# The gate weights of an mLSTM: high and low parts in one tile instead of two

## The chip, the cores and the metric

The kernel runs on one core of one Trainium2 chip. The core has five engines with instruction streams of their own: TensorE (matmuls; its weight loads are shown apart), VectorE, ScalarE, GpSimd and SyncE. They share an on-chip memory, and TensorE writes to accumulator banks. Transfers are issued from the queues of SyncE, ScalarE and GpSimd and are moved by 16 DMA engines. The metric is the time of one execution on the device in microseconds (us), as the median of several.

## The reference

The reference is an encoder trunk of two layers over 256 tokens of width 1024. Each layer is a SwiGLU block, a mixer and another SwiGLU block, each added to its input and normalised. The mixer of the first layer is a bidirectional mLSTM, that of the second a windowed attention. What the change touches is in the mLSTM:

```python
def mlstm_mixer(x, w_in, gate_b, norm_g, w_out):
    p = x @ w_in
    q, k, v, o = ...                     # columns 0 to 3071 of p
    gates = (p[..., 3072:] + gate_b)     # 16 columns: (i, f) x two directions x 4 heads
    h_f = mlstm_chunkwise(q, k, v, gates[0], gates[1])
    h_b = flip(mlstm_chunkwise(flip(q), flip(k), flip(v), flip(gates[2]), flip(gates[3])))
    ...
# in mlstm_chunkwise
    logf = log_sigmoid(f_pre)            # the forget gate, summed along the tokens
    g = cumsum(logf)
    # the input gate i_pre - g and its running maximum weight the scores q k
```

So 16 of the projection's columns are gates; from them come, token after token, the weights of the scores and a stabiliser.

## The kernel before, in words

All matrix products are in float32 precision out of three products in a faster format: each operand is split into a high part (a rounded copy, written by ScalarE) and a low part (the rest, written by VectorE), and `mm3` (lines 619 to 622) adds high by high, high by low and low by high in one bank. The weights come from memory in pieces of 128 x 1024 numbers, over four buffers; for each piece ScalarE writes `w_hi` and VectorE `w_lo`. The profile shows these operations under line 182, the line of the helper through which TensorE, VectorE and ScalarE are called, so one tells them apart by tiles.

The order of the instructions on each engine is written out by the program. In the SwiGLU blocks `Weights.fill` (line 378) decides by modelled times (class `Paced`) when the next piece is split; in the mLSTM the places are fixed by calls of `W.done`. SyncE loads the next piece as soon as a `w_lo` has freed a buffer.

The mLSTM (line 1056) holds the input turned round in `xT` (1024 numbers in 8 strips of 128, by 256 tokens, high and low). Its order is:

- GpSimd clears two weight tiles for the gates, `gw_hi` and `gw_lo` (128 x 8 x 128 each, lines 1065 to 1067). The 16 gate columns of `gw` are split into them (line 1070): the four heads of each gate stand at columns 0, 32, 64 and 96, the rest is zero. So one matmul with these weights lays each gate on partitions of its own.
- v of the first 128 tokens (lines 1090 to 1097), with the turning of the second 128 tokens of the block before put between (`pending`).
- The gates (lines 1099 to 1101): `mm3` for 8 strips, 24 matmuls, into one bank `pg` of 128 x 256.
- The gate chain on VectorE (lines 1102 to 1130): three steps read the bank and add the bias, then come the log-sigmoid (with Exp and Ln on ScalarE), two running sums, `u`, two running maxima, and `ex`. Two small transfers on GpSimd's queue put the maxima into `most` (line 1128).
- Meanwhile TensorE computes v of the second 128 tokens (lines 1132 to 1136); with each half go a split of v and the splits of two more weight pieces.
- Four transposes of `u` and `ex` on TensorE (lines 1138 to 1141), then q and k (lines 1171 to 1185), where GpSimd spreads `most` over the partitions, and after that scores, mixing and the output projection.

`v_lo`, `q_lo` and `w_lo` are low parts written by VectorE; `scan` holds the tiles `fa`, `fe`, `fl` and `fm` of the gate chain, `ig` its input gate. In the rows of the profile both the gate bank and other banks of that pool are called `pw`, those of a second pool `py`.

Of the kernel before, what the change touches and what calls it, by code (L numbers as in the profile page):

```python
# [9 lines left out]
F32 = mybir.dt.float32  # L10
FR = mybir.dt.float32r
AF = mybir.ActivationFunctionType
OP = mybir.AluOpType
# [177 lines left out]
class Weights:  # L191
# [134 lines left out]
    def low(self):  # L326

        nc = self.nc
        i, hi = self.half.pop(0)
        p = self.plan[i]  # L330
        k, scale, raw = p["k"], p["scale"], self.raw[p["word"]]
        lo = self.pool.tile([128, D], FR, name="w_lo", tag="w_lo", bufs=RING)
        if i == 0:
            for j in range(2):
                s_ = slice(j * 512, j * 512 + 512)
                nc.vector.tensor_sub(lo[:, s_], raw[:, s_], hi[:, s_].bitcast(F32))
        elif scale is None:
            nc.vector.tensor_sub(lo, raw, hi.bitcast(F32))
        else:
            nc.vector.scalar_tensor_tensor(lo, raw, scale(), hi.bitcast(F32), op0=OP.mult, op1=OP.subtract)  # L340
        self.parts[i] = (hi.rearrange("p (k f) -> p k f", k=k), lo.rearrange("p (k f) -> p k f", k=k))
        self.fresh = i
        sums = [(i, *sum_) for sum_ in self.after.get(i, ())]
        while sums and not isinstance(sums[0][2], int):
            self.transfer(*sums.pop(0)[1:])
        self.sums += sums
        self.drop(p["word"])
        self.load()
# [98 lines left out]
def trunk_kernel(ctx: ExitStack, tc: tile.TileContext, x, ffn_w_in, ffn_w_out, ln_g, ln_b, ml_w_in, ml_gate_b,  # L447
                 ml_norm_g, ml_w_out, at_w_in, at_sink, at_w_out, out):
    nc = Paced(tc.nc)
# [128 lines left out]
    def load_x(t, h):  # L578
# [3 lines left out]
    xT = (state.tile([128, 8, S], FR, name="xT_hi", tag="xT_hi"),  # L582
          state.tile([128, 8, S], FR, name="xT_lo", tag="xT_lo"))
# [19 lines left out]
    gw = consts.tile([128, 8, 16], F32, name="gw")  # L603
    gbias = consts.tile([128, 1], F32, name="gbias")
# [14 lines left out]
    def mm3(o, l, r, start, stop, onto=False):  # L619
        nc.tensor.matmul(o, l[0], r[0], start=start, stop=False, skip_group_check=onto)  # L620
        nc.tensor.matmul(o, l[0], r[1], start=False, stop=False, skip_group_check=onto)
        nc.tensor.matmul(o, l[1], r[0], start=False, stop=stop, skip_group_check=onto)

    def pair(p, *idx):
        return p[0][idx], p[1][idx]

    def wbank(shape=(128, 512)):
        return psum.tile(list(shape), F32, name="pw", tag="pw", bufs=4)
# [4 lines left out]
    A = slice(None)  # L633
# [4 lines left out]
    def split_evac(dst, src, scale=None, high=None, wait=False):  # L638
        if scale is None:
            (high or nc.scalar.copy)(dst[0], src)  # L640
            low = lambda: nc.vector.tensor_sub(dst[1], src, dst[0].bitcast(F32))
            if wait:
                W.when_ready(low, dst[0])
            else:
                low()
        else:
            nc.scalar.activation(dst[0], src, AF.Copy, scale=scale)
            nc.vector.scalar_tensor_tensor(dst[1], src, scale, dst[0].bitcast(F32), op0=OP.mult, op1=OP.subtract)
# [407 lines left out]
    def mlstm(l, n, pending, last):  # L1056
        with ExitStack() as ph:
            pool = ph.enter_context(tc.tile_pool(name="mlstm", bufs=1))
            tile_ = lambda shape, dt, name, **kw: pool.tile(shape, dt, name=name, tag=kw.pop("tag", name), **kw)

            def both(shape, name, tags=None, bufs=1):
                return tuple(tile_(shape, FR, name + e, tag=(tags or name) + e, bufs=bufs) for e in ("_hi", "_lo"))

            va = [both([128, 4, 258], f"v{t}") for t in range(2)]
            gwi = (tile_([128, 8, 128], FR, "gw_hi", tag="h0"), tile_([128, 8, 128], FR, "gw_lo", tag="h1"))
            for p in gwi:
                nc.gpsimd.memset(p.bitcast(F32), 0.0)
            for g in range(4):
                c = 64 * (g % 2) + 32 * (g // 2)
                split_evac(pair(gwi, A, A, slice(c, c + 4)), gw[:, :, 4 * g:4 * g + 4])  # L1070
            for t in range(2):
                for p, one in zip(va[t], (1.0, 0.0)):
                    nc.gpsimd.memset(p[:, :, 256:258].bitcast(F32), one)
            most = tile_([128, 2, S], F32, "most")
            ones = tile_([64, 32], F32, "ones")[:, 0:1]
            nc.gpsimd.memset(ones, 1.0)

# [20 lines left out]
            nc.scalar.preload_act_table_set("natural_log_exp_and_others")  # L1098
            pg = wbank((128, S))
            for k in range(8):  # L1100
                mm3(pg, pair(gwi, A, k), pair(xT, A, k), k == 0, k == 7)
            scan = tile_([128, 4, S], F32, "scan", tag="sg")
            fa, fe, fl, fm = [scan[0:64, n_] for n_ in range(4)]
            ig = tile_([64, S], F32, "ig")
            nc.vector.tensor_scalar(fa, pg[64:128], gbias[64:128], None, op0=OP.add)
            nc.vector.tensor_scalar(fm, pg[64:128], gbias[64:128], 0.0, op0=OP.add, op1=OP.min)
            nc.vector.tensor_scalar(ig, pg[0:64], gbias[0:64], None, op0=OP.add)
            nc.vector.scalar_tensor_tensor(fa, fm, 2.0, fa, op0=OP.mult, op1=OP.subtract)
            nc.scalar.activation(fe, fa, AF.Exp)
            nc.scalar.activation(fl, fe, AF.Ln, bias=1.0)  # L1110
# [60 lines left out]
            for m in range(2):  # L1171
                for g in range(2):
                    pieces = W.take(2)
                    p = wbank((128, 2, S))
# [419 lines left out]
    for j, (kind, l, i, n) in enumerate(stages):  # L1594
        last = j == len(stages) - 1
        bound[0] = j
        nc.filler = W.fill if kind == "ffn" else None
        if kind == "ffn":
            pending = ffn(l, i, n, pending, last)
        elif kind == "mlstm":  # L1600
            pending = mlstm(l, n, pending, last)
        else:
            pending = attn(l, n, pending, last)
# [29 lines left out]
```

## Time and profile before

| | before |
|---|---|
| median of 3 runs | 911.12 us (910.35 to 911.18) |
| the profiled execution | 910.79 us, its span 909.1 us |
| TensorE busy | 900.3 us (99%), 4427 matmuls |
| VectorE busy | 799.6 us (88%) |
| ScalarE busy | 570.3 us (63%) |
| GpSimd busy | 152.1 us (17%) |
| granted TensorE clock | 0.999 |

A row of a timeline gives the start in us from the span's beginning, the duration, the engine, the line, the operation and its tiles (written <- read), the number of instructions merged into the row, and in brackets how long the engine had been idle and what ended that. A row of a group gives the count, the busy time in us and the mean duration of one in ns.

### The profile page before, as it was taken

What the parts mean: (1) busy time and instruction counts of PE and PEld (TensorE: products, weight loads), DVE (VectorE), ACT (ScalarE), POOL (GpSimd) and SP (SyncE); (2) the same over time, 40 slices, a digit from 0 to 9 for tenths busy, and PEclk for the clock granted to TensorE, in tenths of its full rate; (3) what the DMA queues carried; (4) which work ended last, traced back from release to release, by engine and by line L of the source; (5) the groups of instructions that cost most, each with busy time, mean ns of one, the idle gap of its engine ahead of it and who ended that gap; (6) DMA issues with size and microseconds to landing.
All of it is one profiled execution on the core that took longest, in us unless ns stands there. A gap on an engine that the chain in (4) does not pass through costs nothing.

```text
span 909.1 us, 12461 instructions
## 1 busy us (share of the span) xinstructions
PE 900.3 (99%) x4427; PEld 749.5 (82%) x4427; DVE 799.6 (88%) x961; ACT 570.3 (63%) x785; POOL 152.1 (17%) x190
## 2 busy tenths in 40 slices
PE   9999999999999999999999999999999999999996
PEld 7888888889988888888888888888886788888885
DVE  6999999886799898999988899998868789899986
ACT  5776777356664666776636677765568556676760
POOL 0111123113211011211011112110325301111110
PEclk9999999999999999999999999999999999999999
DMA  8999998546637898998868889986444587899851
GB/s 290 367 330 249 287 276 217 164 138 183 212 106 247 297 237 235 292 278 242 236 197 279 254 248 280 281 220 216 140 140 140 170 294 219 202 296 281 251 140 47
DMA packets 100703, 208.53 MB, mean 229 GB/s; under 512 B 6904, under 2 KB 21264, under 8 KB 100640
## 3 DMA queue, kind: packets, MB, share of 16 engines
q1 hardware_dynamic: 82368, 173.04, 54.4%
q0 software_dynamic: 17696, 33.65, 22.2%
q10 hardware_dynamic: 576, 1.05, 0.3%
q8 instruction: 35, 0.57, 0.2%
q14 instruction: 28, 0.23, 0.1%
HBM read 206.65 MB, written 1.05 MB: 228 GB/s over the span
## 4 chain that ended last, share of the span: by engine, by line
PE 98%; DVE 1%; issue 0%; DVEq 0%; POOL 0%; POOLq 0%
PE pw L182 63%; PE py L182 35%; DVE w_lo L182 0%; DVE x L182 0%; DVE stats L182 0%; DVE e L182 0%; DVE s_raw L182 0%; DVEq L1629 0%; DVE mv L182 0%; POOL ji L597 0%; DVE ident L182 0%; DVE rs L182 0%; DVEq L182 0%; POOLq L597 0%; POOLq L1620 0%
## 5 line engine op out<-in xcount | busy, mean ns | idle before, releaser
L182 DVE TENSOR_TENSOR w_lo<-w_raw,w_hi 128x1024 fp32r<-128x1024 f32 (+1 forms) x213 | 255.8, 1222 | 25.4 <-ACT w_hi L182 23.5
L182 ACT CAST w_hi<-w_raw 128x1024 fp32r<-128x1024 f32 (+1 forms) x213 | 218.9, 1050 | 77.1 <-PE py L182 22.2
L182 DVE TENSOR_TENSOR w_lo<-s_raw,w_hi 128x1024 fp32r<-128x1024 f32 x192 | 228.7, 1220 | 18.8 <-ACT w_hi L182 18.7
L182 ACT CAST w_hi<-s_raw 128x1024 fp32r<-128x1024 f32 x192 | 196.6, 1054 | 58.8 <-PE py L182 25.0
L182 PE MATMUL pw<-w_hi,xT_hi 128*128 128x512 f32 x480 | 189.4, 396 | 0.0
L182 PE MATMUL pw<-w_hi,xT_lo 128*128 128x512 f32 x480 | 186.9, 391 | 0.0
L182 PE MATMUL pw<-w_lo,xT_hi 128*128 128x512 f32 x480 | 186.7, 390 | 0.1
L123 POOL DMA_DIRECT2D s_raw<-in_ffn_w_in_dram x64 | 77.4, 1211 | 484.0 <-DVE s_raw L182 222.3
L182 PE MATMUL py<-w_hi,h_hi 128*128 128x512 f32 x349 | 138.2, 396 | 0.0
L182 PE MATMUL py<-w_hi,h_lo 128*128 128x512 f32 x349 | 136.2, 390 | 0.0
L182 PE MATMUL py<-w_lo,h_hi 128*128 128x512 f32 x349 | 136.0, 390 | 0.0
L182 PEld LDWEIGHTS pw<-w_lo,xT_hi 128*128 128x128 f32 x480 | 90.3, 188 | 18.8 <-DVE w_lo L182 1.3
L182 PEld LDWEIGHTS pw<-w_hi,xT_lo 128*128 128x128 f32 x480 | 90.1, 188 | 19.1
L182 PEld LDWEIGHTS pw<-w_hi,xT_hi 128*128 128x128 f32 x480 | 90.1, 188 | 17.2
L182 PE MATMUL pw<-w_hi,S_lo 128*128 128x512 f32 x256 | 99.7, 389 | 0.0
L182 PE MATMUL pw<-w_lo,S_hi 128*128 128x512 f32 x256 | 99.7, 389 | 0.0
L182 PE MATMUL pw<-w_hi,S_hi 128*128 128x512 f32 x256 | 99.7, 389 | 0.0
L182 DVE TENSOR_TENSOR s_raw<-s_raw,s_raw 128x1024 f32<-128x1024 f32 x64 | 76.8, 1220 | 0.3
L182 PEld LDWEIGHTS py<-w_hi,h_lo 128*128 128x128 f32 x349 | 65.5, 188 | 14.0
L182 PEld LDWEIGHTS py<-w_lo,h_hi 128*128 128x128 f32 x349 | 65.7, 188 | 13.0
L182 PEld LDWEIGHTS py<-w_hi,h_hi 128*128 128x128 f32 x349 | 65.6, 188 | 12.8
L182 PEld LDWEIGHTS pw<-w_lo,S_hi 128*128 128x128 f32 x256 | 48.1, 188 | 10.0
(203 smaller groups left out, 1099.0 us busy)
## 6 DMA issues: line engine op xcount, KB each, us to landing
s_raw<-in_ffn_w_in_dram SPq DMA_DIRECT2D x96, 512.0 KB, 8.0
w_raw<-in_ffn_w_out_dram SPq DMA_DIRECT2D x88, 512.0 KB, 6.2
w_raw<-in_ffn_w_in_dram SPq DMA_DIRECT2D x64, 512.0 KB, 5.6
s_raw<-in_ffn_w_in_dram POOLq DMA_DIRECT2D x64, 512.0 KB, 8.2
w_raw<-in_ml_w_in_dram SPq DMA_DIRECT2D x24, 512.0 KB, 4.4
w_raw<-in_ffn_w_in_dram SPq DMA_DIRECT2D x32, 256.0 KB, 6.1
w_raw<-in_at_w_in_dram SPq DMA_DIRECT2D x12, 512.0 KB, 4.8
w_raw<-in_ml_w_out_dram SPq DMA_DIRECT2D x8, 512.0 KB, 3.8
```

The source lines that it names most:

```text
L123: self.nc.gpsimd.dma_start(ap, source, accum_op=OP.add)
L182: r = f(out, *args, **kw)
```

## The change

The two gate weight tiles become one, `gw_both`: the high parts of a gate stay in their four columns, and the low parts stand in the four columns beside them. So two matmuls for each strip (these weights by the high and by the low part of `xT`) give all products, 16 matmuls instead of 24; the product of low by low comes in too. The rows of the bank that belong to low parts lie four partitions further down. ScalarE copies the bank to `ga`, a transfer on ScalarE's own queue moves rows 4 to 127 of `ga` to rows 0 to 123 of `gl`, and VectorE adds `ga`, `gl` and the bias in the first steps of the gate chain. `ga` and `gl` share a new tile `both_rows` in the room that `gw_lo` had; GpSimd clears `gl`. The minimum for the log-sigmoid now reads the sum instead of the bank.

```diff
-            gwi = (tile_([128, 8, 128], FR, "gw_hi", tag="h0"), tile_([128, 8, 128], FR, "gw_lo", tag="h1"))
-            for p in gwi:
-                nc.gpsimd.memset(p.bitcast(F32), 0.0)
+            gwi = tile_([128, 8, 128], FR, "gw_both", tag="h0")
+            nc.gpsimd.memset(gwi.bitcast(F32), 0.0)
             for g in range(4):
                 c = 64 * (g % 2) + 32 * (g // 2)
-                split_evac(pair(gwi, A, A, slice(c, c + 4)), gw[:, :, 4 * g:4 * g + 4])
+                split_evac((gwi[:, :, c:c + 4], gwi[:, :, c + 4:c + 8]), gw[:, :, 4 * g:4 * g + 4])
...
+            both_rows = tile_([128, 4, 256], F32, "both_rows", tag="h1")
+            gl = both_rows[:, 1]
+            nc.gpsimd.memset(gl, 0.0)
...
             for k in range(8):
-                mm3(pg, pair(gwi, A, k), pair(xT, A, k), k == 0, k == 7)
+                for e in range(2):
+                    nc.tensor.matmul(pg, gwi[:, k], xT[e][:, k], start=k == e == 0, stop=k == 7 and e == 1)
+            ga = both_rows[:, 0]
+            nc.scalar.copy(ga, pg)
+            nc.nc.scalar.dma_start(gl[0:124], ga[4:128])
...
-            nc.vector.tensor_scalar(fa, pg[64:128], gbias[64:128], None, op0=OP.add)
-            nc.vector.tensor_scalar(fm, pg[64:128], gbias[64:128], 0.0, op0=OP.add, op1=OP.min)
-            nc.vector.tensor_scalar(ig, pg[0:64], gbias[0:64], None, op0=OP.add)
+            nc.vector.scalar_tensor_tensor(fa, ga[64:128], gbias[64:128], gl[64:128], op0=OP.add, op1=OP.add)
+            nc.vector.tensor_scalar(fm, fa, 0.0, None, op0=OP.min)
+            nc.vector.scalar_tensor_tensor(ig, ga[0:64], gbias[0:64], gl[0:64], op0=OP.add, op1=OP.add)
```

## The prediction

> **What bounds the kernel now.** I read the page first, for the engine that ends last.
>
> ```profile
> span 909.1 us, 12461 instructions
> PE 900.3 (99%) x4427; PEld 749.5 (82%) x4427; DVE 799.6 (88%) x961; ACT 570.3 (63%) x785; POOL 152.1 (17%) x190
> ...
> PE 98%; DVE 1%; issue 0%; DVEq 0%; POOL 0%; POOLq 0%
> ```
>
> TensorE carries the span: it is busy for 99% of it, and 98% of the chain that ended last is its own work. So there is hardly any idle time on TensorE in which a new wait could vanish. A matmul taken away shortens the run by its own slot, and a wait added in front of a TensorE instruction lengthens it. That profiled execution took 910.79 us in all, 1.69 us more than its span and 0.33 us below the median of the three runs, 911.12 us. I make the sum in changes of the span and add it to the median.
>
> Next comes the timeline of TensorE around the gates (start, duration).
>
> ```profile
> 195.22 0.28 PE L182 MATMUL pw<-xT_hi,gw_hi 128*128 128x256 f32 x1
> ...
> 197.94 0.28 PE L182 MATMUL pw<-xT_hi,gw_lo 128*128 128x256 f32 x1
> 198.06 0.40 PE L182 MATMUL pw<-w_hi,xT_hi 128*128 128x512 f32 x1
> ```
>
> The three products of line 1101 for eight k are 24 matmuls from 195.22 to 198.06, one every (198.06 - 195.22) / 24 = 0.118 us; the 0.28 us of a single row overlaps its neighbours. Behind them stand the v projections of the second token tile, and then the four transposes of line 1141, which need the results of the scan. The weight loads show that place:
>
> ```profile
> 208.52 0.19 PEld L182 LDWEIGHTS pw<-w_hi,xT_lo 128*128 128x128 f32 x1
> 209.06 0.20 PEld L182 LDWEIGHTS pw<-ident,ig 64*128 64x128 f32 x2 [0.35 <-DVE w_lo L182]
> 209.18 0.20 PEld L182 LDWEIGHTS pw<-ident,scan 64*128 64x128 f32 x2
> ```
>
> The pair at 209.18 reads ex, the last result of the gate chain. The 0.35 us ahead of 209.06 is put down to a w_lo that the transposes don't read; I take it for the step from 128 rows to 64 and let it stay. VectorE's timeline shows the chain:
>
> ```profile
> 198.26 0.89 DVE L182 TENSOR_SCALAR scan<-pw,gbias 64x256 f32<-64x256 f32 x2 [0.80 <-PE pw L182]
> 199.19 0.47 DVE L182 TENSOR_SCALAR ig<-pw,gbias 64x256 f32<-64x256 f32 x1
> 199.59 0.40 DVE L182 SCALAR_TENSOR_TENSOR scan<-scan 64x256 f32<-64x256 f32 x1
> 200.48 0.28 DVE L182 TENSOR_SCALAR scan<-scan 64x256 f32<-64x256 f32 x1 [0.48 <-ACT scan L182]
> ...
> 205.58 0.42 DVE L182 SCALAR_TENSOR_TENSOR scan<-scan 64x256 f32<-64x256 f32 x1
> 205.92 0.68 DVE L182 TENSOR_TENSOR v_lo<-pw,v_hi 128x512 fp32r<-128x512 f32 x1
> 206.52 2.34 DVE L182 TENSOR_TENSOR w_lo<-w_raw,w_hi 128x1024 fp32r<-128x1024 f32 x2
> 209.79 0.69 DVE L182 TENSOR_TENSOR v_lo<-pw,v_hi 128x512 fp32r<-128x512 f32 x1 [0.93 <-ACT v_hi L182]
> ```
>
> It begins at 198.26, as soon as the gate matmuls end, and ex is written at 205.58 + 0.42 = 206.00. TensorE loads it at 209.18, so the chain has 3.18 us to spare.
>
> **The change, part by part.**
>
> *The matmuls.* 24 become 16. Eight slots of 0.118 us are 0.95 us, all on the path. What follows on TensorE comes 0.95 us earlier, so the chain's room shrinks as well: ex is now wanted at 209.18 - 0.95 = 208.23.
>
> *The copy.* ScalarE copies the bank before anything else can happen.
>
> ```profile
> 196.11 1.28 ACT L1098 ACT_TABLE_LOAD   x1
> 200.03 0.87 ACT L182 ACTIVATE scan<-scan 64x256 f32<-64x256 f32 x2 [2.63 <-DVE scan L182]
> ```
> ```profile
> L182 ACT COPY v<-pw 128x256 f32<-128x256 f32 x2 | 0.8, 378 | 0.0
> ```
>
> The last gate matmul would end at 197.94 + 0.28 - 0.95 = 197.27; ScalarE is in its table load until 196.11 + 1.28 = 197.39. A copy of this shape takes 0.378 us, so it ends at 197.77 and the transfer is issued at about 197.82 (0.05 us for the handover, an estimate). Copy and issue fall in ScalarE's 2.63 us of idling ahead of 200.03, and its next work, Exp and Ln, belongs to the delayed chain anyway.
>
> *The transfer* moves 124 rows of 1 KB. No row of before shows a transfer between tiles of that size on ScalarE's queue, so I bound it by its neighbours, each row from the list of DMA issues (the last number is us from issue to landing; the first two are the loads issued at 196.90 and at 208.89):
>
> ```profile
> w_raw<-in_ml_w_in_dram SPq DMA_DIRECT2D x1, 512.0 KB, 3.6
> ```
> ```profile
> w_raw<-in_ml_w_in_dram SPq DMA_DIRECT2D x1, 512.0 KB, 5.2
> ```
> ```profile
> most<-scan POOLq DMA_DIRECT2D x2, 4.0 KB, 1.7
> ```
> ```profile
> out_dram<-x SPq DMA_DIRECT2D x1, 256.0 KB, 2.0
> ```
> ```profile
> q1 hardware_dynamic: 528, 0.52, 75.8%
> ```
>
> The last row is the queue while the load of 196.90 ran: 528 packets are 16 x 33, so each of the 16 engines moved 32 rows of 1 KB and one mark of completion. 3.6 us is therefore what 32 such rows on an engine take. 124 rows can't be dealt equally to 16 engines; the largest number up to 16 that divides 124 is 4, and then each of 4 engines moves 31 rows, nearly that load's share. I take the equal deal, and so 3.6 us, from the row it is nearest to by rows on an engine. Bounds: 1.7 us (4 KB, little but latency) and 5.2 us (a load issued 1.1 us behind another, queued with it). The Trainium skill, "DMA: Bandwidth & Descriptors", section "Why a DMA increments its semaphore by 16 and not by 1", states that a transfer issued from ScalarE uses the largest number of engines up to 16 that divides its outermost dimension, and gives 100 partitions on 10 engines as a case; no row of before shows it. By that rule the sum is the one below; by a deal over all 16 it would be 0.81 us less.
>
> *The chain after it.* VectorE waits for the landing at 197.82 + 3.6 = 201.42 and starts at 201.45. Its three first steps took 199.59 - 198.26 = 1.33 us; now they are two sums (0.40 to 0.42 us each, as 199.59 and 205.58) and a minimum of 0.28 us (as 200.48), 1.12 us in all. From start to ex it took 206.00 - 198.26 = 7.74 us; now 7.74 - 0.21 = 7.53. ex is written at 208.98 and seen by TensorE at 209.04, 0.81 us after 208.23. The transposes wait that long, and all of TensorE's work is behind them.
>
> *What else is queued behind the waiting VectorE.* v_lo of 205.92 and the two w_lo of 206.52 slide by about 208.98 - 206.00 = 3.0 us. They were followed by 0.93 us of idling, so the slip shrinks there.
>
> ```profile
> 212.05 1.89 POOL L1160 PARTITION_BROADCAST wt<-most  x2 [5.64 <-issue]
> ```
> ```profile
> 215.50 0.59 ACT L182 CAST q_hi<-pw 128x512 fp32r<-128x512 f32 x1 [1.90 <-PE pw L182]
> ```
>
> The pieces of those two w_lo belong to TensorE's second q group; ScalarE's cast of the first group waits for TensorE until 215.50. So they have until about 215.4, and 206.52 + 2.34 + 3.0 = 211.9 leaves 3.5 us. The banks that v_lo frees are wanted no sooner. The two transfers to `most` slide too, and the broadcasts at 212.05 with them to about 215; they feed score weights that wait in ScalarE behind q_hi and two w_hi, until some 218. Cost nothing; were that cover gone, up to 1 us on ScalarE, which idles 1.90 us there.
>
> *The small ones.* One memset of a weight tile on GpSimd is replaced by one a quarter as large, long before use. The casts and subtractions of the gate weights are as many as before.
>
> **Sum:** -0.95 + 0.81 = -0.14 us, so 911.0 us. Landing sooner than 2.79 us after the issue would cost nothing at all (3.6 - 0.81); beyond that every microsecond of the transfer is one of the run.
>
> **The rivals.**
>
> *All engines share it.* If the 124 rows go over 16 engines, 7 or 8 rows each, the landing is near the 1.7 and 2.0 us rows, below 2.79. Nothing waits and the whole 0.95 us stays: 910.2 us. For it: `out_dram` moved twice the bytes in 2.0 us. Against: it had 128 rows, and 124 don't divide. The skill's same page, section "Anatomy of one DMA", fits about 2.0 us plus bytes over 436 GB/s for GpSimd's path; 127 KB would be 2.3 us, an estimate, and that too is hidden.
>
> *The transfer queues behind a weight load.* The load issued on SP:
>
> ```profile
> 196.90 0.37 SPq L119 DMA_DIRECT2D w_raw<-in_ml_w_in_dram  x1
> ```
> ```profile
> 198.00:200.00 2.00, 2.00 (x11) 1.67 (x11) 1.70 (x4) 0.00 (x0) 0.00 (x0) 1.00 0.88 254
> ```
>
> keeps the DMA engines at a share of 0.88 from 198 to 200 us (the last two columns are that share and GB/s), just when the transfer starts, 0.9 us behind it. In the 5.2 us row the second load stood 1.1 us behind the first. At 5.2 us the transposes wait 0.81 + 1.6 = 2.41 us and the run is slower by 1.46 us: 912.6 us. It turns slower than before from 3.74 us on. Against it: 31 rows on 4 engines don't share the memory behind the load, and part of the load has gone by then.
>
> *The halves in one tile hold each other up.* High parts (ScalarE) and low parts (VectorE) are now written into one tile.
>
> ```profile
> 189.40 0.57 ACT L182 CAST gw_hi<-gw 128x32 fp32r<-128x32 f32 x4 [2.71 <-POOL gw_hi L1067]
> ...
> 193.59 1.07 ACT L182 CAST xT_hi<-py 128x512 fp32r<-128x512 f32 x2 [3.13 <-PE py L182]
> ```
> ```profile
> 192.57 0.49 DVE L182 TENSOR_TENSOR gw_lo<-gw,gw_hi 128x32 fp32r<-128x32 f32 x4
> ```
> ```profile
> 193.75 0.48 PE L182 MATMUL pw<-w_hi,xT_hi 128*128 128x512 f32 x1
> ```
>
> If each cast had to wait for the subtraction ahead of it, the four pairs would alternate from 192.57 to about 194.2, ScalarE's v_hi and xT_hi would be some 1.0 us late, and the copy with them: 912.0 us. Against it: at 193.75 TensorE reads the first tokens' columns of xT_hi while ScalarE writes the second tokens' columns, and doesn't wait.
>
> **How the numbers follow.** Equal deal over 4 engines, 0.50; all 16 engines, 0.27; behind the load, 0.13; alternating halves, 0.05; something outside these, such as another order of weight splits in the later layers, since that order is written from modelled times which shift with the gates, 0.05. The likeliest gives 911.0 us. From 910.0 (the second case less the scatter of the runs) to 912.6 (the third) leaves out about 2 in 10. A difference of 0.2%, 1.8 us, is about what a measurement of this kernel can tell from none. A gain that large has no term here: 0.03. A loss that large needs a landing beyond 5.5 us, or the unknown: 0.08. The rest, 0.89, is within.
>
> **What would show it.** In the changed profile: 16 gate matmuls, 0.118 us apart; the landing on ScalarE's queue about 3.6 us after the issue; VectorE idle for some 4 us ahead of its first gate sum; and TensorE's weight loads waiting about 0.8 us for VectorE's scan tile at line 1141's transposes. No such wait means that all engines shared the transfer. A wait of 2 us or more means that it queued. The prediction is wrong if TensorE waits anywhere else than there, or if later stages run in another order.

## The result and the profile after

The changed kernel takes 912.83 us (median of 9 runs, 911.89 to 914.73), the kernel before 910.59 us (9 runs beside them, 909.94 to 911.47). The ratio is 1.0026, with an interval of 1.0018 to 1.0034: slower by a quarter of a per cent, and above the upper end of the range that I gave. The profiled execution of the changed kernel took 912.83 us with a span of 911.1 us, 2.0 us more than the span before. TensorE's share of the chain that ended last fell from 98% to 94%:

```profile
span 911.1 us, 12450 instructions
...
PE 899.9 (99%) x4419; PEld 747.2 (82%) x4419; DVE 798.8 (88%) x961; ACT 570.3 (63%) x786; POOL 150.5 (17%) x190
...
PE 94%; DVE 2%; DMA 2%; ACT 1%; issue 0%; DVEq 0%; SPq 0%; ACTq 0%
```

TensorE has 8 matmuls fewer (4419 for 4427) and 0.4 us less of work, and yet the span is longer: the time has gone into waiting. TensorE's timeline around the gates in the changed kernel:

```profile
195.48 0.28 PE L182 MATMUL pw<-xT_hi,gw_both 128*128 128x256 f32 x1
...
197.26 0.29 PE L182 MATMUL pw<-xT_lo,gw_both 128*128 128x256 f32 x1
197.38 0.40 PE L182 MATMUL pw<-w_hi,xT_hi 128*128 128x512 f32 x1
```

The 16 gate matmuls take 197.38 - 195.48 = 1.90 us, 0.119 us each; the 24 took 2.84 us. So 0.94 us is gone here, as forecast. This execution came to the gates 0.26 us later than that of before (195.48 for 195.22, most of it from the loads of x at the start); the first matmul behind the gates is therefore 0.68 us earlier than it was (197.38 for 198.06). The weight loads at the next stage:

```profile
207.84 0.19 PEld L182 LDWEIGHTS pw<-w_hi,xT_lo 128*128 128x128 f32 x1
208.44 0.20 PEld L182 LDWEIGHTS pw<-ident,ig 64*128 64x128 f32 x2 [0.41 <-DVE ig L182]
210.32 0.20 PEld L182 LDWEIGHTS pw<-ident,scan 64*128 64x128 f32 x2 [1.68 <-DVE scan L182]
```

The last load of v is still 0.68 us ahead (207.84 for 208.52), the transposes of `u` 0.62 us ahead, and those of `ex` 1.14 us behind (210.32 for 209.18). Between two neighbouring rows TensorE loses 1.76 us, and the bracket says to whom: to VectorE's scan tile, 1.68 us. The steps that led to it, on ScalarE and on VectorE:

```profile
196.37 1.28 ACT L1100 ACT_TABLE_LOAD   x1
197.66 0.37 ACT L182 COPY both_rows<-pw 128x256 f32<-128x256 f32 x1
198.12 1.20 ACTq L1107 DMA_DIRECT2D both_rows<-both_rows  x1
```
```profile
202.73 0.48 DVE L182 SCALAR_TENSOR_TENSOR scan<-both_rows,gbias 64x256 f32<-64x256 f32 x1 [5.00 <-DMA both_rows<-both_rows]
...
209.84 0.42 DVE L182 SCALAR_TENSOR_TENSOR scan<-scan 64x256 f32<-64x256 f32 x1
```

From the issue at 198.12 to VectorE's start at 202.73 are 4.6 us. From there to ex at 209.84 + 0.42 = 210.26 are 7.53 us.

Behind this stage all engines run the instructions in the order of before. TensorE's starts stay 1.1 us and more behind those of before. Two more waits that the trace of before doesn't have stand in this one: 0.4 us for a low part of a weight near 826 us, and 0.6 us for a late xT_lo near 304 us:

```profile
304.22 0.19 PEld L182 LDWEIGHTS pw<-w_hi,xT_lo 128*128 128x128 f32 x1 [0.59 <-DVE xT_lo L182]
```

### The profile page after: what moved, and what is told of

Read it like the earlier page. It is cut to its first block, busy times and chain, and to the rows that moved or that the text cites. A ratio compares the mean times of both kernels' runs of the same rounds, so it can differ in the third digit from the quotient of the medians.

```text
span 911.1 us, 12450 instructions
## 1 busy us (share of the span) xinstructions
PE 899.9 (99%) x4419; PEld 747.2 (82%) x4419; DVE 798.8 (88%) x961; ACT 570.3 (63%) x786; POOL 150.5 (17%) x190
## 4 chain that ended last, share of the span: by engine, by line
PE 94%; DVE 2%; DMA 2%; ACT 1%; issue 0%; DVEq 0%; SPq 0%; ACTq 0%
PE pw L182 61%; PE py L182 34%; DMA w_raw<-in_ffn_w_in_dram 1%; DVE w_lo L182 1%; DVE scan L182 1%; DMA x<-in_x_dram 0%; DMA both_rows<-both_rows 0%; DVE x L182 0%; ACT w_hi L182 0%; DVE xT_lo L182 0%; DVE stats L182 0%; ACT L1100 0%; ACT xT_hi L182 0%; DVE ig L182 0%; DVEq L1635 0%
```

## The experiments

Three questions were open. Does the wait at the transposes make the loss, or the wait at 304 us, which I hadn't foreseen? Why did the transfer land 4.6 us after its issue and not 3.6? And why do the nine runs lie in two heaps, 911.89 to 912.83 and 913.70 to 914.73, where those of before lie in one? Theory A: the 0.94 us are gained and the wait of 1.7 us takes them back; the landing has a fixed part (31 rows on each of 4 engines) and a part from standing behind the weight load. Theory B: the transposes' wait isn't it; the later waits are.

**The changed kernel once more.** No edit.

> The changed kernel once more, for a second trace. Theory: wait at the transposes 1.5 to 1.9 us again, landing 4.3 to 4.8 us after the issue; of what the first trace lost after the transposes (another 0.5 us of TensorE's waits from 302 us on), nothing need come again, since the instructions stand in the same order on each engine. Rival (the late start of the weight splits causes that loss too): the same waits at about 303 us again.

Measured: 913.94 us (11 runs, 912.06 to 914.92) beside 911.18 us, ratio 1.0026 (1.0017 to 1.0034). The wait at the transposes is there again, those at 304 and 826 us are not, so these later waits aren't the cause. Theory B is out. The weight loads of this execution:

```profile
210.69 0.20 PEld L182 LDWEIGHTS pw<-ident,scan 64*128 64x128 f32 x2 [1.68 <-DVE scan L182]
...
211.55 0.33 PEld L182 LDWEIGHTS pw<-xT_hi,w_hi 128*128 128x128 f32 x1
211.76 0.33 PEld L182 LDWEIGHTS pw<-xT_lo,w_hi 128*128 128x128 f32 x1
...
214.60 0.19 PEld L182 LDWEIGHTS pw<-xT_hi,w_hi 128*128 128x128 f32 x1
214.72 0.19 PEld L182 LDWEIGHTS pw<-xT_lo,w_hi 128*128 128x128 f32 x1
```

The same loads follow each other at 0.21 us after the wait and at 0.12 us three microseconds later. The windows show why (columns: stretch, its length, busy time of PE, PEld, DVE, ACT and POOL with the instructions in brackets, granted clock, DMA share, GB/s). First this execution, then the first one of the changed kernel:

```profile
209.00:210.00 1.00, 0.15 (x2) 0.01 (x1) 0.97 (x2) 1.00 (x2) 0.23 (x1) 1.00 0.00 0
210.00:211.00 1.00, 0.31 (x3) 0.24 (x3) 0.96 (x3) 1.00 (x2) 0.95 (x2) 0.98 0.00 0
211.00:214.40 3.40, 3.40 (x17) 3.40 (x17) 3.40 (x5) 0.24 (x1) 0.05 (x1) 0.50 0.25 50
214.40:216.00 1.60, 1.60 (x15) 1.60 (x15) 1.60 (x2) 0.00 (x0) 0.00 (x0) 1.00 0.90 268
```
```profile
211.00:214.40 3.40, 3.40 (x31) 3.40 (x30) 3.40 (x4) 0.00 (x0) 0.00 (x0) 1.00 0.35 89
214.40:216.00 1.60, 1.60 (x16) 1.60 (x15) 1.60 (x3) 0.00 (x0) 0.00 (x0) 1.00 0.97 312
```

In the 3.4 us behind the wait the clock granted is 0.50 in one execution and 1.00 in the other, and TensorE makes 17 matmuls instead of 31. Half of 3.4 us, 1.7 us, is lost on top of the wait. All 20 runs of the changed kernel fall into 10 with a median of 912.42 us and 10 with 914.23 us, 1.8 us apart. The mean granted clock over the span is 0.9977 in the lower ten and 0.9960 in the upper ten; 0.0017 of 911 us are 1.5 us. So the two heaps look like the executions without and with this fall of the clock; the two traces show one of each, the other 18 runs are placed by their time and mean clock alone.

What decides it can be read from the times of the changes. In this execution the granted clock falls at 210.97, rises at 214.38 and falls for good at 907.29, after TensorE's last work: the distances are 1 and 204 times 3.413 us. In the first execution of the changed kernel it falls only at 906.46, and 204 such steps earlier is 210.14. With 122 rows (below) it changes at 211.48, 218.31 and 911.22, 2 and 203 steps apart. So here the clock changes on a fixed beat that doesn't begin with the wait. The steps of this beat that hold the wait, this execution first, then the first one:

```profile
207.56:210.97 3.41, 1.78 (x11) 1.04 (x9) 3.26 (x7) 2.56 (x4) 1.16 (x2) 1.00 0.00 0
```
```profile
206.73:210.14 3.41, 2.04 (x10) 1.30 (x8) 3.26 (x6) 2.46 (x4) 0.70 (x2) 1.00 0.00 0
```

TensorE was busy for 1.78 us of the step before the clock fell, and for 2.04 us of the step that no fall followed. The wait of 1.68 us is the same in both; what differs is mainly its place in the beat. That the limit lies between these two values is inferred from two traces.

The Trainium skill, "TensorE: Matmul & The Clock Gate", section "Part 1: The HAM clock gate (the "warmup" mystery)", states half the clock after at least one idle window of about 3.4 us, with windows of 3413 ns that run freely. The trace agrees on the length of the stretch (3.4 us) and on its running freely; it does not agree that a whole idle window is needed, since TensorE was busy for 1.78 us of the 3.41 us ahead of the fall.

**No transfer at all.** The low parts' rows are not moved, so `gl` stays zero and the gates lack them.

```diff
-            nc.nc.scalar.dma_start(gl[0:124], ga[4:128])
```

> The transfer is left out, so the low parts of the gate weights' products are missing from the gates; copy, sums and the 16 matmuls stay. Theory (the transfer alone costs): no wait at the transposes, 0.9 to 1.0 us faster than before. Rival (the copy on ScalarE, or high and low parts in one tile, or something later in the run costs): no faster than before, or slower by some of the 2.2 us.

Measured: 910.89 us (11 runs), ratio 0.9997 (0.9989 to 1.0006), one heap, and no wait for the scan tile:

```profile
208.87 0.20 PEld L182 LDWEIGHTS pw<-ident,ig 64*128 64x128 f32 x2 [0.35 <-issue]
208.99 0.20 PEld L182 LDWEIGHTS pw<-ident,scan 64*128 64x128 f32 x2
```

The transfer alone makes the loss: about 3 us of median between this kernel and the changed one on the same chip. But the 0.94 us saved shows only as 0.29 us at the median, less than the 0.9 us expected; the interval reaches from 1.0 us faster to 0.5 us slower.

**Another number of rows.** The last low part stands in row 103 of `gl`, so fewer rows can be moved with the same result. 112 divides by 16, 122 only by 2.

```diff
-            nc.nc.scalar.dma_start(gl[0:124], ga[4:128])
+            nc.nc.scalar.dma_start(gl[0:112], ga[4:116])
```

> The transfer moves 112 rows instead of 124; nothing is lost by that, since the last low part stands in row 103. Theory (rows are dealt equally to as many engines as divide their number, and the transposes wait for the landing): 112 = 16 x 7, so 7 rows on each of 16 engines, an issue of about 0.4 us as SP's loads have, a landing 1.7 to 2.3 us after the issue, no wait of the weight loads for VectorE's scan tile, and the 0.95 us of the matmuls stay: faster than before by about 0.9 us, and 2.5 to 3 us below the changed kernel. Rival (a transfer on ScalarE's queue has a fixed price, whatever its rows): landing again about 4.5 us, wait again 1.7 us, time as the changed kernel.

Measured: 911.36 us (11 runs, 910.58 to 911.92), ratio 1.0000 (0.9992 to 1.0009), one heap. ScalarE's issue, the transfer in the list of DMA issues, its queue, and the wait:

```profile
198.72 0.60 ACTq L1107 DMA_DIRECT2D both_rows<-both_rows  x1
```
```profile
q10 hardware_dynamic: 128, 0.11, 6.9%
...
both_rows<-both_rows ACTq DMA_DIRECT2D x1, 112.0 KB, 3.0
```
```profile
209.38 0.19 PEld L182 LDWEIGHTS pw<-ident,scan 64*128 64x128 f32 x2 [0.20 <-DVE scan L182]
```

128 packets are 112 rows and 16 marks of completion: 16 engines. The landing comes after 3.0 us, and 0.20 us of the wait is left. The loss is gone, as the theory had it, but the landing came later than its 1.7 to 2.3 us, and the gain of 0.9 us didn't come. The other kernel:

```diff
-            nc.nc.scalar.dma_start(gl[0:124], ga[4:128])
+            nc.nc.scalar.dma_start(gl[0:122], ga[4:126])
```

> The transfer moves 122 rows, again all that is needed. Theory: 122 = 2 x 61, so 2 engines with 61 rows each; at 0.06 to 0.07 us a row (the 31 rows took 2.16 us) some 4 us instead of 2.2, landing 6.3 to 6.8 us after the issue, and each microsecond more is one more of TensorE's wait: wait about 3.5 to 4 us, slower than the changed kernel by about 2 us. Rival (fixed price, or price by bytes): within 0.2 us of the changed kernel.

Measured: 915.71 us (6 runs, 913.10 to 916.92), ratio 1.0040 (1.0027 to 1.0054). The queue, VectorE's first sum, the waits and a window:

```profile
q10 hardware_dynamic: 124, 0.12, 6.0%
```
```profile
204.59 0.48 DVE L182 SCALAR_TENSOR_TENSOR scan<-both_rows,gbias 64x256 f32<-64x256 f32 x1 [6.37 <-DMA both_rows<-both_rows]
```
```profile
210.30 0.20 PEld L182 LDWEIGHTS pw<-ident,ig 64*128 64x128 f32 x2 [1.78 <-DVE ig L182]
212.18 0.28 PEld L182 LDWEIGHTS pw<-ident,scan 64*128 64x128 f32 x2 [1.68 <-DVE scan L182]
```
```profile
216.00:218.00 2.00, 2.00 (x11) 2.00 (x11) 2.00 (x3) 0.00 (x0) 0.00 (x0) 0.50 0.88 255
```

124 packets are 122 rows and 2 marks: two engines, 61 rows each. VectorE starts 6.0 us after the issue (204.59 - 198.63), a little sooner than expected. The waits add up to 3.46 us, 3.11 us more than the 0.35 us that stand at this place in before. The clock stays at 0.50 for 6.8 us from 211.48 on, two stretches of 3.4 us; 0.7 us of them pass while TensorE still waits, and half of the other 6.1 us is lost, 3.1 us. -0.94 + 3.11 + 3.1 = +5.3 us. Counted from its first gate matmul, this execution ends 5.3 us later than the one of before.

With 124 rows the queue has 128 packets too, 124 rows and 4 marks, and the DMA share while they alone run is 0.27 (shown below), about 4 of 16 engines. So the deal is the one of the prediction: the largest number up to 16 that divides the rows, 4, 2 and 16 here.

**The clock by itself.** The wait stays, but TensorE is kept busy in it: 13 transposes of a constant (the program's own `warm`) between v and the four transposes.

```diff
+            warm(13)
             pt = wbank((128, 2, 2, 64))
```

> The changed kernel with 13 more transposes of the identity on TensorE ahead of line 1141's place, some 1.65 us of work that nobody reads, in the gap that the transfer leaves. Theory (in some executions the granted TensorE clock falls to half after the idle gap of 1.7 us, for one stretch of 3.4 us, and that makes the two groups of the changed kernel's times, 911.9 to 912.8 and 913.7 to 914.9): with the gap filled the clock stays at 1.0 in every execution, the upper group disappears, and the median falls to about 912.4 although TensorE has more to do; the wait for the scan tile shrinks to 0.5 us or less. Rival (the upper group comes from something else, or a late transfer makes it): two groups again, median about 913.5.

Measured: 912.52 us (11 runs, 911.64 to 913.41) beside 911.31 us, ratio 1.0013 (1.0004 to 1.0022). The mean granted clock is 0.997 to 0.999 in all eleven runs (0.995 to 0.997 in the upper ten of the changed kernel), and in the trace it is 1.00 throughout the stage:

```profile
209.08 1.57 PEld L182 LDWEIGHTS py<-ident 128*128 128x128 f32 x13
210.81 0.20 PEld L182 LDWEIGHTS pw<-ident,ig 64*128 64x128 f32 x2 [0.17 <-DVE scan L182]
211.29 0.20 PEld L182 LDWEIGHTS pw<-ident,scan 64*128 64x128 f32 x2 [0.29 <-DVE scan L182]
```

TensorE does 13 matmuls more, and yet this kernel loses 1.2 us against the before beside it, where the changed one lost 2.2 and 2.8 us at its two medians: the clock no longer falls. The lower heap of the changed kernel (912.42 us) lies 1.2 and 1.8 us above the two medians of before.

**The transposes put later.** The block with the four transposes moves behind the first q group, so that TensorE has other work while the chain ends; the transfer keeps its 124 rows.

```diff
-            pt = wbank((128, 2, 2, 64))
...
+                    if m == g == 0:
+                        pt = wbank((128, 2, 2, 64))
+                        for n_, src in enumerate((u, ex)):
+                            for t in range(2):
+                                nc.tensor.transpose(pt[:, n_, t], src[:, tok(t)], ident[:64, :64])
...
```

> The changed kernel, with the four transposes of u and ex put behind the first q group (48 matmuls, 5.7 us) instead of ahead of it; the transfer stays at 124 rows and 4.6 us. Theory (all that is lost is TensorE's wait for the landing and what the clock does with it): no wait, no fall of the clock, so the 16 matmuls show: between 0.9 us faster than before and the same, 2 to 3 us below the changed kernel. Rival (the slip of VectorE's weight splits by 4 us costs by itself): slower than before by 0.5 us or more.

Measured: 911.30 us (11 runs, 910.35 to 913.15), ratio 0.9998 (0.9990 to 1.0007). The transposes wait for nothing:

```profile
213.87 0.20 PEld L182 LDWEIGHTS pw<-ident,ig 64*128 64x128 f32 x2
213.99 0.20 PEld L182 LDWEIGHTS pw<-ident,scan 64*128 64x128 f32 x2
```

The whole loss is gone with the transfer as long as it was. But this isn't faster than before either. In its trace TensorE waits further on, among others here:

```profile
544.51 0.19 PEld L182 LDWEIGHTS py<-w_hi,h_lo 128*128 128x128 f32 x1 [0.64 <-DVE h_lo L182]
```

**What a gate matmul is worth.** Two edits of the kernel before: the gate weights' low parts left out of the products (16 matmuls, no transfer), and all 24 matmuls made twice.

```diff
-                mm3(pg, pair(gwi, A, k), pair(xT, A, k), k == 0, k == 7)
+                for e in range(2):
+                    nc.tensor.matmul(pg, gwi[0][:, k], xT[e][:, k], start=k == e == 0, stop=k == 7 and e == 1)
```

> The kernel before with 16 gate matmuls, nothing else changed: the products of the low parts of the gate weights are left out. Theory (TensorE sets the end from the gates on, so a matmul less is its slot less): 0.95 us faster than before. Rival (a later stretch, where VectorE splits weights without a pause and TensorE waits for a weight's low part at about 564 us, takes part of it back): 0.2 to 0.5 us faster, and that wait at 564 us longer by the rest.

```diff
                 mm3(pg, pair(gwi, A, k), pair(xT, A, k), k == 0, k == 7)
+            for k in range(8):
+                mm3(pg, pair(gwi, A, k), pair(xT, A, k), k == 0, k == 7)
```

> The kernel before with its 24 gate matmuls made twice over, the second set writing over the first: 24 slots more, 2.84 us. Theory (TensorE sets the end): 2.8 us slower than before. Rival (later waits of TensorE absorb a delay): 2.3 us or less slower, with the wait at about 564 us gone.

Measured: eight fewer, 910.73 us (11 runs, 909.89 to 912.69), ratio 0.9995 (0.9986 to 1.0004); 24 more, 914.12 us (6 runs, 913.62 to 914.71), ratio 1.0028 (1.0017 to 1.0040). The 24 cost 914.12 - 911.31 = 2.81 us, their 24 x 0.118 = 2.83 us. The eight give 0.58 us at the median instead of 0.95, and the interval reaches from 1.3 us faster to 0.4 us slower. The trace of that kernel has no wait near 564 us at all, so the rival, a longer wait there, is not what it shows.

**The transfer away from the weight load.** In the changed kernel with the 16 matmuls made twice, the copy and the transfer come some 2 us later, when SyncE's load has nearly ended. The second with 112 rows.

```diff
                     nc.tensor.matmul(pg, gwi[:, k], xT[e][:, k], start=k == e == 0, stop=k == 7 and e == 1)
+            for k in range(8):
+                for e in range(2):
+                    nc.tensor.matmul(pg, gwi[:, k], xT[e][:, k], start=k == e == 0, stop=k == 7 and e == 1)
```

> The changed kernel with its 16 gate matmuls made twice, so that the copy and the transfer of 124 rows come 1.9 us later, when the weight load that SP issues at 197 us has landed. Theory A (the transfer's packets stand behind that load's on the DMA engines, and begin as its last ones go): first packet within 1.2 to 1.4 us of the issue instead of 1.9, and landing 3.5 to 4.0 us after the issue instead of 4.6. Theory B (the price is the transfer's own, an issue of 1.2 us and 31 rows on each of 4 engines): first packet again 1.9 us after the issue, landing again 4.5 to 4.7 us.

> The same delay with 112 rows on 16 engines. Theory A: landing 2.0 to 2.4 us after the issue instead of 3.0. Theory B: 3.0 us again.

The edit of the second is that of 112 rows above. Measured: single times of 913.80 us and 912.72 us beside 911.00 us. SyncE's load, its landing, the transfer's issue and VectorE's start with 124 rows:

```profile
197.60 0.37 SPq L119 DMA_DIRECT2D w_raw<-in_ml_w_in_dram  x1
```
```profile
w_raw<-in_ml_w_in_dram SPq DMA_DIRECT2D x1, 512.0 KB, 3.5
```
```profile
200.39 1.21 ACTq L1110 DMA_DIRECT2D both_rows<-both_rows  x1
```
```profile
204.01 0.48 DVE L182 SCALAR_TENSOR_TENSOR scan<-both_rows,gbias 64x256 f32<-64x256 f32 x1 [5.83 <-DMA both_rows<-both_rows]
```

204.01 - 200.39 = 3.6 us: away from the load the transfer takes what the prediction gave it, and 1.0 us of the 4.6 us goes with the load beside it. With 112 rows it landed after 2.3 us instead of 3.0, and nothing waited. In the changed kernel itself the queues show the same. The load is issued on SyncE at 197.15, 0.97 us ahead of the transfer. In the windows the DMA share falls from 1.06 to 0.27 at about 200.3, and from 200.4 on ScalarE's queue is the only one listed and has 110 of its 128 packets still to come:

```profile
199.50:200.00 0.50, 0.50 (x4) 0.42 (x3) 0.00 (x0) 0.00 (x0) 0.00 (x0) 1.00 1.06 379
200.00:200.50 0.50, 0.50 (x4) 0.42 (x3) 0.00 (x0) 0.00 (x0) 0.00 (x0) 1.00 0.57 180
200.50:201.00 0.50, 0.50 (x4) 0.42 (x3) 0.00 (x0) 0.00 (x0) 0.00 (x0) 1.00 0.27 63
```
```profile
q10 hardware_dynamic: 110, 0.11, 18.8%
```

Its first packet began at 200.05, 1.9 us after the issue; away from the load it was 1.4 us. From the first packet to the last it took 2.1 us (to 202.20); away from the load 1.7 us. So 0.6 us of the 1.0 us is a later start and 0.4 us slower packets. By which mechanism the load does this stays open.

**GpSimd's queue.** The same 124 rows, issued by GpSimd.

```diff
-            nc.nc.scalar.dma_start(gl[0:124], ga[4:128])
+            nc.nc.gpsimd.dma_start(gl[0:124], ga[4:128])
```

> The changed kernel with the transfer of 124 rows on GpSimd's queue, where descriptors are written by software, instead of ScalarE's. Theory (the equal deal over 4 engines belongs to the queues of ScalarE and SP): all 16 engines take part, 124 rows in about 0.6 us, landing 2.5 to 3.2 us after the issue, and a wait for the scan tile of 0.4 us or less. Rival (any queue deals 124 rows to 4 engines): rows again over 1.6 to 2.2 us, wait 1 us or more.

Measured: one time of 910.78 us beside 911.00 us. The transfer landed after 2.8 us, and 0.53 us of waiting is left, a little more than expected. Its first packet came 1.2 us after the issue, while SyncE's load still had 0.6 us of packets to move:

```profile
q0 software_dynamic: 48, 0.13, 6.0%
...
both_rows<-both_rows POOLq DMA_DIRECT2D x1, 124.0 KB, 2.8
```
```profile
209.05 0.20 PEld L182 LDWEIGHTS pw<-ident,scan 64*128 64x128 f32 x2 [0.53 <-DVE scan L182]
```

**Both remedies.** 112 rows and the later transposes.

> Both remedies at once: 112 rows, so 16 engines, and the transposes of u and ex behind the first q group. Theory (with no wait the matmuls' 0.95 us are left, less what a later stretch takes back): 0.3 to 0.9 us faster than before. Rival (whatever is gained ahead of 560 us is given back to the stretch in which VectorE splits weights without a pause): within 0.2 us of before, as the kernel with the late transposes alone.

Both edits stand above. Measured: 910.75 us (11 runs, 910.21 to 912.66) beside 911.00 us, ratio 1.0001 (0.9992 to 1.0010). No TensorE wait in its stage; counted from the first gate matmul, its trace is 1.0 us ahead of the one of before near 682 us and 0.8 us at the end. The timed runs don't show it: at the median it is 0.25 us, less than the theory asked. So no version here beats the kernel before by more than a measurement can tell.

## Why the prediction was wrong, point by point

- **The matmuls** (-0.95 us) were right: 0.94 us in the trace, and 24 added ones cost their full slots.
- **The place and the chain** were right: the wait is at line 1141's transposes, for the scan tile; the chain took the 7.53 us I gave; the later splits slid without a wait of TensorE there, and the order stayed. Waits elsewhere, which I had named as a sign of being wrong, stand in the first trace (304 and 826 us) and not in the second.
- **The deal** over 4 engines was right, by the marks of completion, and so were its 3.6 us for a transfer that stands alone. That the number fits is luck in part: I took it from a load whose issue took 0.37 us on SyncE, while ScalarE's took 1.21 us, so the same sum has other parts.
- **The step that failed is the landing**: "I take the equal deal, and so 3.6 us". It was 4.6 us, because SyncE's load was still moving: the first packet came 0.6 us later than alone, and the packets took 0.4 us longer. I had the load at a DMA share of 0.88 in front of me and made of it a separate case with 0.13 and a price of 5.2 us, while the two add up: the deal's price and 1.0 us beside the load. The issue stood 0.30 us later than I put it, 0.26 of it from the later start of this execution and 0.04 from a handover of 0.09 us (198.12 after the copy's end at 198.03) where I had estimated 0.05. The wait became 1.7 us instead of 0.81. "A wait of 2 us or more means that it queued" was too coarse a test: it queued, and the wait was 1.7 us.
- **A second step failed, the price of the wait**: "beyond that every microsecond of the transfer is one of the run", and so a loss of 1.8 us was to need "a landing beyond 5.5 us". It came at 4.6 us. In one of two traces the clock fell to half for 3.4 us behind the wait and cost 1.7 us again, as much as the wait itself; by times and mean clocks this happened in about half of the twenty executions and lifts the upper ten to 914.23 us.

The sum by the runs: -0.94 for the matmuls and +1.76 for the stage make +0.8 us; the clock adds 1.8 us in ten runs of twenty, 0.9 us on average; together +1.7 us. The mean of the 20 runs is 913.36 us, about 2.4 us above the runs of before beside them. What is missing, some 0.7 us, is also missing in the kernels without the wait (no transfer, fewer matmuls, later transposes, both remedies), which should be 0.95 us faster and are so by 0.0 to 0.6 us. A wait near 564 us, 0.54 us in before, comes and goes from trace to trace, and the kernel with later transposes waits at 544 us. The spans of single traces can't settle this, since the first gate matmul itself starts anywhere from 195.22 to 196.50 us. Counted from it, TensorE is 1.1 and 1.0 us ahead of before near 682 us in the two traces without the wait at 564 us (fewer matmuls, both remedies), and only 0.4 and 0.3 us in two that have 0.99 and 0.87 us of it (no transfer, 112 rows). So in these traces the gain goes into that wait. But 24 added matmuls had 0.93 us of it too and were not softened by it: what sets it stays open.

## What to carry to other kernels

A transfer's price is its own time by the rows on each engine that it is dealt to, plus what a load in flight adds (here 1.0 us, with 2.3 us of the load's packets still to come at the issue): add both before comparing it with the room, and on ScalarE's queue choose a number of rows that 16 divides. Where TensorE is the bound, a wait can cost twice its length, as one of 1.7 us did here, because the clock may fall behind it; put other matmuls into it, or the waiting ones behind them. And when runs of one kernel lie in two heaps, look at the granted clock in windows of both.

## What the runs showed of the hardware that I hadn't expected

- An idle time of 1.7 us on TensorE (0.5 us more ahead of two transposes before it) was followed by a granted clock of 0.50 for 3.4 us in one of two traces, and by times and mean clocks in about ten of twenty executions; 3.5 us of waits (with two transposes between) by 0.50 for 6.8 us.
- The granted clock changed only in whole steps of 3.413 us counted from its other changes. TensorE busy for 1.78 us of such a step was followed by half the clock, busy for 2.04 us was not; in the kernel with 122 rows, 1.21 us was followed by two steps at half.
- ScalarE's issue of the transfer took 1.20 us with 124 rows and 1.21 us with 122, but 0.60 us with 112; it ran beside nothing that waited for ScalarE.
- A transfer on ScalarE's queue began its packets only as the load on SyncE's queue ended, although the two are different queues: 1.9 us after the issue instead of 1.4. GpSimd's transfer began its own 1.2 us after the issue, with 0.6 us of the load still to come.
- GpSimd's queue moved the same 124 rows in 48 packets, 31 of them larger than 2 KB, and landed them 2.8 us after the issue, 1.8 us sooner than ScalarE's queue did.
